# Hybrid conv/S5 block on one Trainium2 core: the u_s quarters are scaled, stored and reloaded one at a time, and the last g_s product moves ahead of two "so" products

## The chip, the cores and the metric

The kernel runs on one core of a Trainium2 chip. A core has four compute engines that run side by side, each with its own instruction stream in fixed order: TensorE (PE in the profile; its weight loads are shown as PEld), VectorE (DVE), ScalarE (ACT) and GpSimd (POOL). SyncE (SP) computes nothing here; it issues all DMA transfers of this kernel, also in fixed order, and a DMA whose data or buffer isn't ready holds what stands behind it in SP's stream. Engines wait for each other through semaphores.

The metric is device time in microseconds, lower is better. Three runs of the kernel before gave 844.75, 844.65 and 843.45 us, a median of 844.65 us.

## The reference

One decoder layer on x of shape 1024 x 1024, in float32. Cut to what matters:

```python
h = rms_norm(x, pre_g)
proj = h @ w_in
conv_in, z_c, u_s, z_s, g_c, g_s = split(proj)         # widths 2048, 1024, 512, 512, 1024, 1024
ca, cb = split(conv_in)
cu = causal_depthwise_conv(ca * sigmoid(cb), conv_w, conv_b)      # 31 taps
cu = silu(layer_norm(cu))
conv_out = (cu * silu(z_c)) @ w_conv_out
y = gelu(s5_mimo(u_s, ...))              # 32 groups of 16 channels, a 64-dim complex state each
y = y * sigmoid(y @ w_glu + b_glu)
ssm_out = (y * silu(z_s)) @ w_ssm_out
merged = sigmoid(g_c) * conv_out + sigmoid(g_s) * ssm_out
out = x + rms_norm(merged @ w_out, post_g)
```

The state recurrence of `s5_mimo` is linear: s_t = A s_(t-1) + B u_t, y_t = Re(C s_t) + D u_t.

## The kernel before, in words

**Tiling.** Activations lie as channel x time: a tile is 128 channels by 1024 time steps (4 KB in each partition, 512 KB in all). Every matrix product is done in three passes with operands split into a high and a low part (`h` and `l`, type fp32r): high times high, high times low, low times high. So a product with 8 blocks of 128 in its inner dimension ("a unit") is 48 matmuls of 128x128 by 128x512, and one with 4 blocks ("glu", "so") is 24. A weight comes in by DMA as a raw tile (`wload`, L687 to L694, two raw buffers), is copied to its high part by ScalarE (`wsplit_h`, L703), and the low part is the difference, taken by VectorE (`wsplit_l`, L711). When `wsplit_l` is done, the raw buffer is free, and the next `wload` is issued. The weights come in the order of the list `order`, two units ahead.

**Stages.** First come the normalisation and the products for u_s: three of its four 128-channel tiles together (L848), then the fourth (L867). A copy of each to SBUF is `usT[m]` (L185). Then the list `seq` (L757 to L761) gives the order of the products on TensorE: pairs `cb`, `ca` (convolution gate), `gc`, `zc`, `glu`, `zs`, pairs of `gs` and `so`, at last eight `co` products; after them comes the output product (L1017). What follows a product (sigmoid, multiplication, store) is put off by `post` and emitted by `flush` at step k = 1 of the next product (k = 0 with 4 blocks).

**u_s.** `us_out(m)` (L187 to L195) multiplies `usT[m]` by the norm factors on VectorE, stores it to the DRAM tensor `us_scratch` with one DMA of 512 KB, and reads it back in another layout with eight DMAs of 64 KB into `U[m]` (L195): 8 groups of 16 channels, 8 consecutive time steps folded into the partitions. The first of the eight reads must wait on SP until the store has landed. The function is called for m = 0 to 3 in a row, before the first product of `seq`.

**S5.** `s5_chain` first works out parameters (`s5_params`), then handles the four quarters (8 groups each) one after the other in `s5_quarter(c, P)`: it builds `RT` on VectorE (L392 to L396), transposes it on TensorE (`rp`, L399), multiplies it with `U[c]` (`ep`, L411), works out a small product `kp` (L432, L433), sines and cosines on ScalarE, a scan (L471), swaps halves of tiles through DMA (`E2`, `Zw`), and at the end has `yp` (L489, L490, which reads `U[c]` again), a GELU, a transpose `yq` (L497) and `y32[c]`.

**What sets the order.** All instructions are emitted by one Python program, and each engine runs its own in the order of emission. A planner, the object `clk` of class `Clock`, decides where side work goes: `clk.now` is the time planned for TensorE (1.296 us for each step k of a product), `clk.dve` the time up to which VectorE is planned to be busy. `clk.fg(cost)` adds cost to `clk.dve`. `clk.tick` moves `now` on and then runs one step of the first task in its list that is due (`max(t[1], self.dve) <= self.now`, L658), and starts over from the top of the list. A task is a generator that yields (cost, delay); with cost 0 the next due time is counted from its last due time. Tasks are `s5`, `conv` (the taps of the convolution, L537), `st` and `ln` (the layer norm), and `cu`.

**The "cu" entry.** The marker `("cu", 0)` in `seq` flushes what was put off, forces the convolution and the layer norm to be emitted, and adds a task with eight steps (L973, L974): each copies one tile to its high part (ScalarE) and takes the difference (VectorE). The first `co` product forces what is left of them (L981).

**Tiles.** Activation tiles come from one pool of 21 buffers (`NT = 21`, `T(name)`).

Of the kernel before, what the change touches and what calls it, by code (L numbers as in the profile page):

```python
# [35 lines left out]
def tile_hybrid_block(  # L36
# [40 lines left out]
    def T(name, dt=F32):  # L77
        return tp.tile([128, 1024], dt, tag="T", name=name)

    def PS(name, tag):  # L80
        return ps.tile([128, 1024], F32, tag=tag, name=name)

    def f32(t):
        return t.bitcast(F32)
# [76 lines left out]
    def x_spread(rb):  # L161
        for t in range(8):
            PE.matmul(rb[:, t * 128:(t + 1) * 128], lhsT=r8t[:, t:t + 1].to_broadcast([128, 128]), rhs=ident,
                      start=True, stop=True)
        rbc = T("rbc")
        A.activation(out=rbc, in_=rb, func=AF.Copy)
        return rbc
# [15 lines left out]
    def us_copy(m, p):  # L183
        usT[m] = T(f"usT{m}")
        A.activation(out=usT[m], in_=p, func=AF.Copy)  # L185

    def us_out(m, rbc):  # L187
        u = usT.pop(m)
        V.tensor_tensor(out=u, in0=u, in1=rbc, op=ALU.mult)
        clk.fg(1.2)  # L190
        nc.sync.dma_start(out=us_scr[m], in_=u)
        usU[m] = T(f"U{m}")
        src = us_scr[m].rearrange("(g h) (t n) -> t h g n", g=8, t=8)
        for t in range(8):
            nc.sync.dma_start(out=usU[m][16 * (7 - t):16 * (8 - t)].rearrange("p (g n) -> p g n", g=8), in_=src[t])  # L195
# [321 lines left out]
    def conv_taps(c, ext):  # L517
        acc[c] = T(f"acc{c}")
        av = acc[c].rearrange("p (i e n) -> p e i n", i=4, e=2)
        ye, yo = av[:, 0], av[:, 1]  # L520
        pp = T(f"pp{c}").rearrange("p (e i n) -> p e i n", e=2, i=4)
        p0, p1 = pp[:, 0], pp[:, 1]

        def src(e, r):
            a_, b_ = divmod(r, 4)
            return ext[:, e, 3 - b_:7 - b_, 4 - a_:132 - a_]

        A.activation(out=p0, in_=src(0, 0), func=AF.Copy, scale=cw[:, c, 0:1])  # L528
        A.activation(out=p1, in_=src(1, 0), func=AF.Identity, scale=cw[:, c, 1:2], bias=nb1[:, c:c + 1])
        A.activation(out=yo, in_=src(2, 0), func=AF.Copy, scale=hs[:, c, 0:1])  # L530
        yield 0.0, 2.2
        for r in range(1, 16):
            for e, o, w in ((0, p0, cw[:, c, 2 * r:2 * r + 1]), (1, p1, cw[:, c, 2 * r + 1:2 * r + 2]),
                            (2, yo, hs[:, c, r:r + 1])):
                if e == 1 and r == 15:
                    continue
                V.scalar_tensor_tensor(out=o, in0=src(e, r), scalar=w, in1=o, op0=ALU.mult, op1=ALU.add)  # L537
                yield 0.665, 0
        V.scalar_tensor_tensor(out=ye[:, 1:4, :], in0=p0[:, 1:4, :], scalar=b2[:, c:c + 1], in1=p1[:, 0:3, :],
                               op0=ALU.add, op1=ALU.add)  # L540
        V.scalar_tensor_tensor(out=yo, in0=p0, scalar=-1.0, in1=yo, op0=ALU.mult, op1=ALU.add)
        yield 1.2, 0
        V.scalar_tensor_tensor(out=ye[:, 0, 1:128], in0=p0[:, 0, 1:128], scalar=b2[:, c:c + 1],
                               in1=p1[:, 3, 0:127], op0=ALU.add, op1=ALU.add)
        V.tensor_scalar(out=ye[:, 0, 0:1], in0=p0[:, 0, 0:1], scalar1=chn[:, 0, c:c + 1], scalar2=None,
                        op0=ALU.add)
        V.tensor_tensor(out=yo, in0=yo, in1=p1, op=ALU.subtract)
        yield 1.1, 0
# [3 lines left out]
    def conv_chain():  # L552
        while conv_left[0]:
            if not conv_q:
                yield 0.0, 0.5
                continue
            c, e = conv_q[0]
            for v in conv_taps(c, e):
                yield v
            conv_q.pop(0)  # L560
            conv_left[0] -= 1
            clk.add(f"st{c}", ln_stat(c))
            yield 0.0, 0.0
# [8 lines left out]
    def ln_stat(c):  # L572
        yield 0.0, 3.5
        p = PS(f"lnp{c}", "aux")
        for t in range(8):
            PE.transpose(p[:, t * 128:(t + 1) * 128], acc[c][:, t * 128:(t + 1) * 128], ident)  # L576
        clk.now += 0.9
        yield 0.0, 2.0
        for t in range(8):
            V.bn_stats(out=st8[:, t, c, :], in_=p[:, t * 128:(t + 1) * 128])  # L580
            if t % 4 == 3:
                yield 0.9, 0.0
        stat_left[0] -= 1
        yield 0.0, 0.0
# [86 lines left out]
    clk = Clock()  # L671
# [80 lines left out]
    pairs = [[("cb", c), ("ca", c)] for c in range(8)]  # L752
    fill = [("gc", m) for m in range(8)] + [("zc", m) for m in range(8)]
    zs, glu = [("zs", m) for m in range(4)], [("glu", m) for m in range(4)]
    gso = [[("gs", m), ("so", m)] for m in range(8)]
    gc, zc = fill[0:8], fill[8:16]
    seq = pairs[0] + gc[0:1] + pairs[1] + gc[1:8] + pairs[2] + zc[0:2] + pairs[3] + zc[2:4]  # L757
    seq += [("yhl", 0)] + glu + zs[0:1] + pairs[4] + zs[1:4] + [("y2", 0)] + pairs[5] + gso[0] + gso[1] + pairs[6]
    seq += gso[2] + gso[3] + pairs[7] + zc[4:6] + gso[4] + zc[6:8] + gso[5] + gso[6] + gso[7][0:1] + [("cu", 0)]
    seq += gso[7][1:2]  # L760
    seq += [("co", m) for m in range(8)]  # L761
    NOW = ("yhl", "y2", "cu")
    order += [("us", 3)] + [u for u in seq if u[0] not in NOW] + [("wo", k) for k in range(WHL)]
# [17 lines left out]
    def s5_chain():  # L781
        yield from s5_params(P5)
        for c in range(4):
            while not P5_ready[0]:
                yield 0.0, 0.5
            yield from s5_quarter(c, P5)
        for c in range(4):
            yh[c], yl[c] = T(f"yh{c}", F32R), T(f"yl{c}", F32R)
            A.activation(out=yh[c], in_=y32[c], func=AF.Copy)
            V.tensor_tensor(out=yl[c], in0=y32[c], in1=f32(yh[c]), op=ALU.subtract)  # L790
            yield 1.15, 0
        s5_done[0] = True
        yield 0.0, 0.0
# [9 lines left out]
    rbc = None  # L803
    for k in range(8):
        if k == 0:
            us_weights(2)
            load_xt(6)
            load_xt(7)
            for t in range(3):
                load_x(t)  # L810
            clk.add('s5', s5_chain())
# [32 lines left out]
        for n_, (m, i) in enumerate([(m, i) for i in range(3) for m in range(3)]):  # L844
# [8 lines left out]
            if k == 6 and n_ == 5:  # L853
                rbc = x_spread(PS("rb", "aux"))
# [19 lines left out]
            wsplit_l()  # L874
        clk.tick(1.296)
    us_copy(3, usp[3])
    for m in range(4):
        us_out(m, rbc)
    P5_ready[0] = True
    clk.add('conv', conv_chain())  # L880

    mgh, mgl = {}, {}
# [15 lines left out]
    for u in seq:  # L898
        kind, m = u
# [244 lines left out]
```

## Time and profile before

| quantity | value |
|---|---|
| median of three runs | 844.65 us (843.45 to 844.75) |
| the profiled execution's own time | 844.35 us |
| span in the trace of that execution | 842.6 us |
| TensorE busy | 819.7 us, 97% of the span |
| weight loads busy | 681.1 us, 81% |
| VectorE busy | 622.1 us, 74% |
| ScalarE busy | 279.6 us, 33% |
| GpSimd busy | 25.8 us, 3% |
| DMA | 90.77 MB, 108 GB/s on average |
| mean granted TensorE clock | 0.994 |

Times in the trace count from the start of the span. An engine's row in a timeline has its start, its length, the source line, the operation with its output and inputs, how often it was repeated, and in brackets the idle time of the engine before it and what ended this. "SPq" is a DMA being issued by SP: its length is that of the issue, and the landing comes later. A list of waits sums idle time of an engine by the line that waited and the line that released it. The table of windows gives busy time of each engine in a stretch, and the clock that TensorE was granted as a share of full speed.

### The profile page before, as it was taken

Reading aid. Unit: us, or ns where it says so; the run is one execution under the profiler, and the core shown is the slowest. Engines: PE = TensorE matmul, PEld = TensorE weight load, DVE = VectorE, ACT = ScalarE, POOL = GpSimd, SP = SyncE. Lnnn points to the kernel's source line nnn. Section 1 sums busy time; section 2 is a strip of 40 time slices with the busy share of each in tenths; the row PEclk is TensorE's granted clock in tenths of the full one; section 3 lists DMA queues with packets and bytes.
Section 4 is the critical chain, followed back from the end, with each engine's and each line's share of the span. In section 5 each row is a group of like instructions: output and inputs, shape, how many; then the busy total and the mean of one; then the engine's idle time right before and its main releaser. Section 6 shows DMA issues by size and latency. Waiting matters only on the chain.

```text
span 842.6 us, 9753 instructions
## 1 busy us (share of the span) xinstructions
PE 819.7 (97%) x3856; PEld 681.1 (81%) x3856; DVE 622.1 (74%) x902; ACT 279.6 (33%) x301; POOL 25.8 (3%) x26
## 2 busy tenths in 40 slices
PE   6999799999999999999999999999999999999996
PEld 5887588888888888888888888888888788888885
DVE  4689499889799899988889869589593644452242
ACT  5762344354515453323231121033162411122121
POOL 3400000000000000000000000000000000000010
PEclk9999899999999999999999999999999999999999
DMA  9704432332323302210112202112343443325142
GB/s 343 273 26 147 153 90 75 103 111 101 87 77 100 90 26 99 76 51 26 51 38 87 78 24 100 75 64 101 137 171 129 153 172 145 140 76 189 51 175 100
DMA packets 35181, 90.77 MB, mean 108 GB/s; under 512 B 8305, under 2 KB 13041, under 8 KB 35137
## 3 DMA queue, kind: packets, MB, share of 16 engines
q1 hardware_dynamic: 35136, 90.17, 31.2%
q8 instruction: 30, 0.49, 0.2%
q14 instruction: 15, 0.11, 0.0%
HBM read 65.90 MB, written 18.87 MB: 101 GB/s over the span
## 4 chain that ended last, share of the span: by engine, by line
PE 81%; DVE 10%; ACT 3%; DMA 2%; issue 2%; SPq 1%; DVEq 0%; POOLq 0%; ACTq 0%
PE pgs L736 10%; PE pzc L736 10%; PE pco L736 10%; PE po L1017 10%; PE pcb L736 8%; PE pca L736 8%; PE pzs L736 5%; PE pso L736 5%; PE usp L848 4%; PE pgc L736 4%; PE pgl L736 3%; DVE pp L537 1%; DVE xl L176 1%; DMA Zw<-Zs 1%; PE lnp L576 1%
## 5 line engine op out<-in xcount | busy, mean ns | idle before, releaser
L537 DVE SCALAR_TENSOR_TENSOR pp<-ext,cw,pp 128x512 f32<-128x512 f32 x232 | 165.4, 745 | 10.5 <-ACT pp L528 10.5
L537 DVE SCALAR_TENSOR_TENSOR acc<-ext,hs,acc 128x512 f32<-128x512 f32 x120 | 89.3, 744 | 0.0
L1017 PE MATMUL po<-wox,mgh 128*128 128x512 f32 x192 | 52.3, 389 | 0.0
L736 PE MATMUL pcb<-xh,wh_cb 128*128 128x512 f32 x128 | 40.7, 399 | 5.6 <-ACT wh_cb L703 5.6
L513 ACT ACTIVATE ext<-ext 128x1179 f32<-128x1179 f32 x8 | 9.5, 1190 | 104.7 <-DVE ext L512 104.7
L1017 PEld LDWEIGHTS po<-wox,mgh 128*128 128x128 f32 x192 | 36.0, 188 | 7.5
L736 PE MATMUL pca<-xh,wl_ca 128*128 128x512 f32 x128 | 39.7, 391 | 1.2 <-DVE wl_ca L711 1.1
L736 PE MATMUL pco<-cuh,wl_co 128*128 128x512 f32 x128 | 39.5, 390 | 1.3 <-DVE wl_co L711 1.3
L736 PE MATMUL pgc<-xh,wh_gc 128*128 128x512 f32 x128 | 40.5, 397 | 0.0
L736 PE MATMUL pcb<-xh,wl_cb 128*128 128x512 f32 x128 | 40.3, 396 | 0.0
L736 PE MATMUL pcb<-xl,wh_cb 128*128 128x512 f32 x128 | 40.3, 397 | 0.0
L736 PE MATMUL pzc<-xh,wh_zc 128*128 128x512 f32 x128 | 40.3, 396 | 0.0
L736 PE MATMUL pzc<-xh,wl_zc 128*128 128x512 f32 x128 | 39.6, 390 | 0.5 <-DVE Sx L482 0.5
L736 PE MATMUL pca<-xh,wh_ca 128*128 128x512 f32 x128 | 39.8, 392 | 0.1
L1033 DVE TENSOR_TENSOR o<-po,postg 128x1024 f32<-128x1024 f32 (+1 forms) x9 | 10.0, 1106 | 40.3 <-ACT q L1032 40.3
L736 PE MATMUL pgc<-xl,wh_gc 128*128 128x512 f32 x128 | 39.5, 390 | 0.0
L736 PE MATMUL pgs<-xh,wh_gs 128*128 128x512 f32 x128 | 39.5, 390 | 0.0
L736 PE MATMUL pzc<-xl,wh_zc 128*128 128x512 f32 x128 | 39.5, 390 | 0.0
L736 PE MATMUL pgc<-xh,wl_gc 128*128 128x512 f32 x128 | 39.5, 389 | 0.0
L736 PE MATMUL pca<-xl,wh_ca 128*128 128x512 f32 x128 | 39.4, 389 | 0.0
L736 PE MATMUL pco<-cuh,wh_co 128*128 128x512 f32 x128 | 39.4, 389 | 0.0
L736 PE MATMUL pco<-cul,wh_co 128*128 128x512 f32 x128 | 39.4, 389 | 0.0
(267 smaller groups left out, 1773.2 us busy)
## 6 DMA issues: line engine op xcount, KB each, us to landing
xt<-in_xt_dram SPq DMA_DIRECT2D x8, 512.0 KB, 6.3
xin<-in_x_dram SPq DMA_DIRECT2D x8, 512.0 KB, 9.8
wr_cb<-in_w_in_dram SPq DMA_DIRECT2D x8, 512.0 KB, 3.3
wr_ca<-in_w_in_dram SPq DMA_DIRECT2D x8, 512.0 KB, 3.2
wr_gc<-in_w_in_dram SPq DMA_DIRECT2D x8, 512.0 KB, 3.3
gc_scratch<-gct SPq DMA_DIRECT2D x8, 512.0 KB, 2.6
wr_zc<-in_w_in_dram SPq DMA_DIRECT2D x8, 512.0 KB, 3.2
zc_scratch<-zct SPq DMA_DIRECT2D x8, 512.0 KB, 2.6
```

Source lines behind the costliest of these rows:

```text
L176: V.tensor_tensor(out=xl[:, k, :], in0=xn, in1=f32(xh[:, k, :]), op=ALU.subtract)
L513: A.activation(out=ext[:, :, 0:3, 1:132], in_=ext[:, :, 4:7, 0:131], func=AF.Copy)
L537: V.scalar_tensor_tensor(out=o, in0=src(e, r), scalar=w, in1=o, op0=ALU.mult, op1=ALU.add)
L576: PE.transpose(p[:, t * 128:(t + 1) * 128], acc[c][:, t * 128:(t + 1) * 128], ident)
L736: PE.matmul(p[:, js(j)], lhsT=lhs[:, ks], rhs=rhs(k, j), start=st, stop=sp_)
L848: PE.matmul(usp[m][:, js_], lhsT=lhs[:, kk[m]], rhs=rhs[:, k, js_], start=(k == 0 and i == 0), stop=(k == 7 and i == 2))
L1017: PE.matmul(p[:, js(j)], lhsT=lhs[k][:, s], rhs=rhs[k][:, js(j)], start=st, stop=sp_)
L1033: V.tensor_tensor(out=o[:, s], in0=p, in1=pog[:, s], op=ALU.mult)
```

## The change

The edit has two parts.

1. `us_out` keeps the multiplication and the store. The eight reads become a function of their own, `us_in(m)`. Quarter 0 is scaled, stored and read where it was before. Quarters 1 to 3 are scaled and stored by a new task `us`, one per step, with due times 8 us apart. It stands in the task list after `s5` and ahead of `conv`. The reads of quarter c (1 to 3) are emitted at the start of `s5_quarter(c)`.
2. In `seq`, the last `gs` product (`gs` 7) stands ahead of the `so` products 6 and 7; the marker `cu` follows it, so both of these `so` products come between the marker and the first `co` product, where one did before.

```diff
@@ us_out
         V.tensor_tensor(out=u, in0=u, in1=rbc, op=ALU.mult)
         clk.fg(1.2)
         nc.sync.dma_start(out=us_scr[m], in_=u)
+
+    def us_in(m):
         usU[m] = T(f"U{m}")
         src = us_scr[m].rearrange("(g h) (t n) -> t h g n", g=8, t=8)
         for t in range(8):
@@ seq
-    seq += gso[2] + gso[3] + pairs[7] + zc[4:6] + gso[4] + zc[6:8] + gso[5] + gso[6] + gso[7][0:1] + [("cu", 0)]
-    seq += gso[7][1:2]
+    seq += gso[2] + gso[3] + pairs[7] + zc[4:6] + gso[4] + zc[6:8] + gso[5] + gso[6][0:1] + gso[7][0:1] + [("cu", 0)]
+    seq += gso[6][1:2] + gso[7][1:2]
     seq += [("co", m) for m in range(8)]
@@ s5_chain
         for c in range(4):
             while not P5_ready[0]:
                 yield 0.0, 0.5
+            if c:
+                us_in(c)
             yield from s5_quarter(c, P5)
@@ after the fourth u_s product
     us_copy(3, usp[3])
-    for m in range(4):
-        us_out(m, rbc)
+    us_out(0, rbc)
+    us_in(0)
+
+    def us_rest():
+        for m in range(1, 4):
+            us_out(m, rbc)
+            yield 0.0, 8.0
+
     P5_ready[0] = True
+    clk.add('us', us_rest())
     clk.add('conv', conv_chain())
```

## Prediction, made before the changed kernel was run

> **What bounds the kernel now.** I read the page first. TensorE is busy for 819.7 of 842.6 us, so nearly all of what an edit of order can win lies in the 22.9 us in which it isn't, or in which its clock is down.
>
> ```profile
> PE 819.7 (97%) x3856; PEld 681.1 (81%) x3856; DVE 622.1 (74%) x902; ACT 279.6 (33%) x301; POOL 25.8 (3%) x26
> ```
>
> The list of waits of TensorE names those that another engine or a DMA ended (total, times, longest):
>
> ```profile
> PE usp L848 <- ACT wush L132: 7.2, 1, 7.2
> PE pcb L736 <- ACT wh_cb L703: 5.6, 1, 5.6
> PE pco L736 <- DVE wl_co L711: 1.3, 1, 1.3
> PE pca L736 <- DVE wl_ca L711: 1.1, 1, 1.1
> PE pzc L736 <- DVE Sx L482: 0.5, 1, 0.5
> ```
>
> The 7.2 us are the start, which the change doesn't touch. Three waits are within its reach: 5.6, 1.3 and 1.1 us. What is behind the first shows in the timelines of SP and of the engines around 91 us (start, length, line, instruction, in brackets the idle time before it):
>
> ```profile
> 63.79 0.33 SPq L191 DMA_DIRECT2D us_scratch<-usT  x1
> 66.45 3.65 SPq L195 DMA_DIRECT2D U<-us_scratch  x8
> 70.20 0.37 SPq L191 DMA_DIRECT2D us_scratch<-usT  x1
> ...
> 84.14 0.34 SPq L191 DMA_DIRECT2D us_scratch<-usT  x1
> 87.77 3.62 SPq L195 DMA_DIRECT2D U<-us_scratch  x8
> 91.48 0.37 SPq L693 DMA_DIRECT2D wr_cb<-in_w_in_dram  x1
> ```
>
> ```profile
> 94.91 1.06 ACT L703 ACTIVATE wh_cb<-wr_cb 128x1024 fp32r<-128x1024 f32 x1 [10.81 <-DMA wr_cb<-in_w_in_dram]
> 96.00 1.23 DVE L711 TENSOR_TENSOR wl_cb<-wr_cb,wh_cb 128x1024 fp32r<-128x1024 f32 x1 [10.73 <-ACT wh_cb L703]
> 96.02 1.22 PE L736 MATMUL pcb<-xh,wh_cb 128*128 128x512 f32 x2 [5.58 <-ACT wh_cb L703]
> ```
>
> The reader is to see one queue. Each quarter of u_s costs SP a store, the wait until it has landed, and eight issues: about 7 us, four times, from 63.79 to 91.4 us. The weight of the second `cb` stands behind all four. So ScalarE idles 10.81 us, VectorE 10.73 us and TensorE 5.58 us.
>
> The idle time has a second price. The table of windows (busy time of PE, PEld, DVE, ACT and POOL, then clock, DMA share, GB/s) shows the clock at half after the gap:
>
> ```profile
> 84.00:96.00 12.00, 6.43 (x33) 5.08 (x31) 1.24 (x3) 1.19 (x3) 0.95 (x1) 0.95 0.56 187
> 96.00:101.30 5.30, 5.28 (x12) 4.12 (x13) 5.30 (x6) 3.71 (x5) 0.00 (x0) 0.50 0.42 158
> 103.10:106.00 2.90, 2.90 (x15) 2.19 (x13) 2.90 (x6) 1.97 (x2) 0.00 (x0) 1.00 0.14 31
> ```
>
> Twelve matmuls took 5.3 us at clock 0.50; at full clock they take half, so 2.65 us were lost.
>
> The Trainium skill (TensorE: Matmul & The Clock Gate, Part 1) says that after an idle window of about 3.4 us the clock falls to half, and that about 3.4 us of work bring it back. The trace agrees on the half, not on the length: it was down for 5.3 us. By the rule's 3.4 us the loss would be 1.7 us, and the sum below would come out 0.95 us higher; I keep the row.
>
> **Part one: the quarters of u_s.** What goes from the front is three multiplications on VectorE, three stores and 24 reads on SP. Nothing is saved in all: the same instructions come later.
>
> ```profile
> 62.55 4.63 DVE L189 TENSOR_TENSOR usT<-usT,rbc 128x1024 f32<-128x1024 f32 x4
> 67.09 1.22 DVE L711 TENSOR_TENSOR wl_ca<-wr_ca,wh_ca 128x1024 fp32r<-128x1024 f32 x1
> 68.36 0.72 PE L736 MATMUL pca<-xh,wl_ca 128*128 128x512 f32 x2 [1.12 <-DVE wl_ca L711]
> ```
>
> *First term, -1.12 us.* The low part of `ca` follows the multiplications at once. With three of four (4.63 x 3/4 = 3.5 us) gone from before it, it is ready 3.5 us sooner, and the wait of 1.12 us goes with 2.4 us to spare.
>
> *Second term, -5.58 us.* SP is free after the reads of quarter 0, at 66.45 + 3.65 = 70.1 us. The raw buffer that `wr_cb` needs is free when `wl_ca` ends (68.3 before, some 65 now). So the load goes out at about 70.1 instead of 91.48 us and lands at about 73.5 (91.48 to 94.91 is 3.4 us). ScalarE then reaches `wh_cb` when what stands ahead of it is done; that is the copy of `ext`:
>
> ```profile
> 82.91 1.19 ACT L513 ACTIVATE ext<-ext 128x1179 f32<-128x1179 f32 x1 [13.23 <-DVE ext L512]
> ```
>
> So `wh_cb` ends by 84.10 + 1.06 = 85.2 us. TensorE wants it at 96.02 - 5.58 - 1.12 = 89.3 us. The wait is gone with 4 us of cover; were the cover gone too, `wl_cb` would be late next, which VectorE has done by about 86.4 us for a use at 90.2.
>
> *Third term, -2.65 us*, the half clock, which falls with the gap.
>
> *Where the work goes.* By the planner's rule `s5` comes first whenever it is due, and it is due as soon as VectorE is planned free, except in its own delays. Counting the planner's costs by hand, the delay after `RT` of quarter 0 takes the first multiplication, the delay after `otmp` the second, the delay after `ta` the third: with products `gc` 0 and the second `cb`, at roughly 79 to 93 us. VectorE has the room, since it idled 10.73 us right there and the three need 3.5 us. What is queued behind them on VectorE are S5 and conv steps; `wl_cb` keeps the 4 us above. Each store waits on SP for its multiplication, emitted in the same step; behind it stand weight loads that have most of a unit until use.
>
> The reads, eight issues of 3.65 us, now stand at the start of quarters 1 to 3, past the weight loads and the stores of `gc`, `E` and `Zw`. They can delay a load by 3.65 us; loads go out two units ahead, and a unit of 24 or 48 matmuls takes 5.44 us or twice that. `U` itself must be there for `ep`. Quarter 2 is the tightest:
>
> ```profile
> 637.81 5.44 PE pso L736 x24
> 265.75 1.78 PE ep L411 x16
> 202.03 1.22 DVE L382 TENSOR_TENSOR RT<-PR,bb 128x1024 f32<-128x1024 f32 x1
> 202.14 0.33 SPq L693 DMA_DIRECT2D wr_ca<-in_w_in_dram  x1
> 207.54 1.04 ACT L401 ACTIVATE R<-rp 128x1024 f32<-128x1024 f32 x1 [1.24 <-PE rp L399]
> 212.07 1.03 ACT L416 ACTIVATE Et<-ep 128x1024 f32<-128x1024 f32 x1 [2.56 <-PE ep L411]
> DMA to landing us min/median/max: 2.2/2.5/3.3
> ```
>
> The reads would go out right behind `wr_ca`, at 202.5 us, be issued by 206.2 and land 2.5 us later (last row, the landing times of `U`), at 208.7. The other input of `ep`, `R`, is ready at 208.6. `ep` ended near 212.0 and takes about 1.8 us, so it began at 210.2. That leaves 1.5 us: no cost, with a bound of +1 us for each of three quarters if the order shifts. POOL has nothing moved past it.
>
> *Does VectorE follow?* TensorE would be 9.35 us earlier from 103 us on (1.12 + 5.58 + 2.65). From 96 to 164 us VectorE is nearly full:
>
> ```profile
> 96.00:164.00 68.00, 67.98 (x373) 57.23 (x374) 64.03 (x82) 27.12 (x28) 0.95 (x1) 0.96 0.32 97
> 164.87 0.28 DVE L446 TENSOR_TENSOR kr<-kp,dmt 16x128 f32<-16x128 f32 x1 [2.71 <-ACT kr L445]
> 230.67 1.23 DVE L711 TENSOR_TENSOR wl_ca<-wr_ca,wh_ca 128x1024 fp32r<-128x1024 f32 x1 [4.34 <-ACT wh_ca L703]
> 243.69 0.73 PE L736 MATMUL pzc<-xh,wl_zc 128*128 128x512 f32 x2 [0.55 <-DVE Sx L482]
> ```
>
> At 164.87 us it waits for `kr`, that is for TensorE's `kp`. Up to there it had idled 10.73 us, 4.0 us in the window (68.00 - 64.03, the start of the 2.71 us included) and the rest of the 2.71, 0.9 us: 15.6 us. With `kp` 9.35 us earlier it can still afford 6.2 us, and it had 1.8 us of other idle time (4.0 + 0.9 - 2.71 = 2.2 at most). So it follows with about 4 us to spare. From there to the wait of 0.55 us at 243.69 the chain of waits runs through VectorE, ScalarE and DMA, starting from `kp`; it moves as a whole. Since S5 stands in other places against the products, I allow new small waits: +0.3 us, with bounds -0.55 (the present one goes) and +4.5 (the first rival).
>
> **Part two: gs 7 ahead of so 6 and so 7.** Nothing is added or removed.
>
> ```profile
> 654.17 1.03 ACT L951 ACTIVATE gst<-pgs 128x1024 f32<-128x1024 f32 x1 [10.70 <-PE pgs L736]
> 655.09 1.05 ACT L703 ACTIVATE wh_co<-wr_co 128x1024 fp32r<-128x1024 f32 x1
> 657.12 3.50 DVE L974 TENSOR_TENSOR cul<-acc,cuh 128x1024 fp32r<-128x1024 f32 x3 [11.94 <-ACT cuh L973]
> 660.54 1.22 DVE L711 TENSOR_TENSOR wl_co<-wr_co,wh_co 128x1024 fp32r<-128x1024 f32 x1
> 661.81 0.50 PE L736 MATMUL pco<-cuh,wl_co 128*128 128x512 f32 x1 [1.33 <-DVE wl_co L711]
> 634.09 0.68 DVE L711 TENSOR_TENSOR wl_so<-wr_so,wh_so 128x512 fp32r<-128x512 f32 x1
> ```
>
> Now the last `so` (5.44 us) covers the sigmoid, `wh_co`, the first `cuh`, three `cul` and `wl_co`, and TensorE still waits 1.33 us. In the changed order the same chain comes after `gs` 7, but the weight behind the three `cul` is that of `so` 7, half as large: VectorE needs 0.68 instead of 1.22 us, and ScalarE, in the same ratio, 0.46 us less than 1.05. So `wl_so` ends at 660.54 - 0.46 + 0.68 = 660.76 for a use at 661.81 - 1.33 = 660.48: a wait of 0.3 us. By the planner's count `wl_co` then stands behind two `cul`, the multiplication of `so` 6 and another `cul` (4.6 us), so it ends at 660.7 + 4.6 + 1.2 = 666.5, for a use 5.44 us after 660.76, at 666.2: another 0.3 us. So the term is -1.33 + 0.6 = -0.7 us, between -1.33 (no wait) and +0.5 (each wait twice what I count, and one more).
>
> **Sum.** The profiled execution took 844.35 us (0.3 below the median of the runs, inside their spread). 844.35 - 1.12 - 5.58 - 2.65 - 0.7 + 0.3 = 834.6 us; with half of the 0.3 for the median, 834.8 us.
>
> **Rivals.** *One: VectorE gives part of it back.* With TensorE earlier it must not idle more than 6.2 us up to `kp`; one more pair of waits as long as the 4.34 us at 230.67 (ScalarE held in its sine chain) makes 2.2 + 8.7 = 10.9, 4.7 too many. For it: VectorE is 94% busy there, and the interleaving is new. Against: since 106 us TensorE waited 0.55 us in all until 654. It gives 834.8 + 4.6 = 839.4 us. Chance 0.17.
>
> *Two: slower. The reads at a quarter's start come late.* SP takes its stream in order; if the buffer for `U` or a store ahead holds the reads for 5 us beyond what I found, `ep` waits, TensorE stands, and the loads behind are late too. The gap at 96 us shows the price of one such stop: 5.58 + 2.65 = 8.2 us. One stop gives 843.0, two of three quarters 851.2 us; it decides from about 10 us on. Against it: `R` takes as long as `U`, and the reads find their store landed for 40 us or more. Chance 0.05.
>
> The Trainium skill (DMA: Bandwidth & Descriptors, the section on the anatomy of one DMA) says that a wait for a semaphore takes place on the issuing sequencer before dispatch. The rows of SP above agree: the reads start at 66.45, 2.7 us after their store, and nothing else is issued in between.
>
> *Three: the change doesn't do what it says.* If a store of the new task comes to stand ahead of `wr_cb` on SP and its multiplication is late, the second and third terms stay: 844.35 - 1.12 - 0.7 = 842.5 us. Chance 0.04.
>
> **How the numbers follow.** Forecast 0.74 (in it, some 0.05 for a better result near 833), the rivals 0.17, 0.05, 0.04. The likeliest is 834.8 us. Low end: both unknowns at their good bound, 834.8 - 0.85 - 0.65, and 0.5 us of spread: 832.8. High end: the first rival and 1 us: 840.4. Beyond it lie two and three, and a larger give-back. A run tells no change from one of less than 0.2%, 1.7 us. Faster: 0.74 + 0.17 and most of three, 0.92. Same: 0.03. Slower: 0.05.
>
> **What would show it.** In the new trace: `wr_cb` issued near 70 us; no gap in TensorE near 90 us, and clock 1.00 from 84 to 106; `ep` of quarter 0 starting near 90 instead of 101.3; all three stores between 75 and 95 us; reads of `U` in four places; no wait of TensorE for `R` or `U`; two waits of some 0.3 us near 651 and 656 us. I'm wrong if TensorE shows a new wait of over 1 us between 95 and 330 us, above all at `ep` or `Sx`.

## The result, and the profile after

| quantity | before | after |
|---|---|---|
| median of the runs of one comparison | 844.7 us (4 runs, 843.45 to 845.08) | 835.01 us (4 runs, 834.77 to 835.94) |
| profiled execution's own time | 844.35 us | 834.89 us |
| span | 842.6 us | 833.1 us |
| mean granted clock | 0.994 | 0.998 |

The changed kernel is faster: ratio 0.989, interval 0.9873 to 0.9907. The median came out 0.2 us from the 834.8 us on record. How much of that is understanding and how much is errors that cancelled is the matter of the sections below.

The page of the changed kernel shows the same work in a shorter span (busy us, share, instructions):

```profile
PE 816.3 (98%) x3856; PEld 678.2 (81%) x3856; DVE 622.6 (75%) x902; ACT 279.4 (34%) x301; POOL 26.4 (3%) x26
```

The counts of TensorE, VectorE, ScalarE and GpSimd are those of before, so nothing was removed. TensorE's 3.4 us less of busy time are mostly matmuls that no longer run at half clock.

TensorE's waits on other engines in the changed kernel (total, times, longest):

```profile
PE usp L852 <- ACT wush L132: 7.2, 1, 7.2
PE pgs L738 <- ACT gst L962: 1.2, 1, 1.2
PE lnp L578 <- DVE st L582: 0.7, 2, 0.5
PE pso L738 <- DVE wl_so L713: 0.4, 1, 0.4
PE pgl L738 <- DVE wl_glu L713: 0.3, 1, 0.3
```

The start is untouched. The waits of 5.6, 1.3, 1.1 and 0.5 us of before (`wh_cb`, `wl_co`, `wl_ca`, `Sx`) are all gone. Behind the edit are four that were not there: 1.2 us at `gs` 6, 0.7 us in the layer norm, 0.4 us at an `so` and 0.3 us at the `glu` product.

SP's queue in the changed kernel, where the four blocks of store, wait and eight reads stood (start, length of the issue, line, transfer):

```profile
63.22 0.33 SPq L191 DMA_DIRECT2D us_scratch<-usT  x1
65.88 3.65 SPq L197 DMA_DIRECT2D U<-us_scratch  x8
69.62 0.38 SPq L695 DMA_DIRECT2D wr_cb<-in_w_in_dram  x1
...
80.45 0.33 SPq L191 DMA_DIRECT2D us_scratch<-usT  x1
86.91 0.33 SPq L191 DMA_DIRECT2D us_scratch<-usT  x1
91.19 0.56 SPq L191 DMA_DIRECT2D us_scratch<-usT  x1
121.95 3.79 SPq L197 DMA_DIRECT2D U<-us_scratch  x8
178.10 3.80 SPq L197 DMA_DIRECT2D U<-us_scratch  x8
234.20 4.00 SPq L197 DMA_DIRECT2D U<-us_scratch  x8
```

The load of `wr_cb` goes out at 69.62 instead of 91.48 us, right behind the reads of quarter 0. The other three stores follow their multiplications at 80 to 92 us, and the other reads stand about 56 us apart, one block for each quarter of S5. What this did on the engines, from the timelines of ScalarE and VectorE and the table of windows (busy time of PE, PEld, DVE, ACT, POOL, then clock, DMA share, GB/s):

```profile
83.44 1.04 ACT L705 ACTIVATE wh_cb<-wr_cb 128x1024 fp32r<-128x1024 f32 x1
...
187.56 1.03 ACT L403 ACTIVATE R<-rp 128x1024 f32<-128x1024 f32 x1 [2.02 <-PE rp L401]
```

```profile
63.11 1.22 DVE L713 TENSOR_TENSOR wl_ca<-wr_ca,wh_ca 128x1024 fp32r<-128x1024 f32 x1
79.21 1.22 DVE L189 TENSOR_TENSOR usT<-usT,rbc 128x1024 f32<-128x1024 f32 x1
85.66 1.22 DVE L189 TENSOR_TENSOR usT<-usT,rbc 128x1024 f32<-128x1024 f32 x1
89.27 1.22 DVE L189 TENSOR_TENSOR usT<-usT,rbc 128x1024 f32<-128x1024 f32 x1
```

```profile
84.00:96.00 12.00, 12.00 (x85) 10.12 (x84) 9.60 (x10) 6.18 (x9) 0.03 (x1) 1.00 0.65 214
96.00:101.30 5.30, 5.30 (x25) 4.40 (x24) 5.22 (x7) 4.03 (x4) 0.00 (x0) 1.00 0.20 36
```

The same two windows as before the change: TensorE is busy in all of 84 to 96 us, where it had 6.43 us, and the clock is 1.00 from 96 to 101.3, where it was 0.50. 25 matmul records instead of 12 fit into those 5.3 us.

The chain of waits of both kernels gives the gain up to that place. Before, then after (start, length, what, count):

```profile
37.31 1.78 PE rb L163 x16
101.50 1.88 PE ep L411 x16
```

```profile
36.47 2.05 PE rb L163 x16
87.06 1.78 PE ep L413 x16
90.22 2.72 PE pcb L738 x12
```

In the kernel before, `ep` of quarter 0 ended at 101.50 + 1.88 = 103.38 us, and TensorE had done two steps of the second `cb` by then. With the change it has done `ep` and these two steps at 90.22 + 2.72 = 92.94 us. That is 10.44 us earlier. Of these, 0.57 us were there from the start: `rb` ended at 38.52 instead of 39.09 us, ahead of anything that was edited. The front of part one is therefore worth 9.87 us.

### The profile page after: what moved, and what is told of

Its sections match the earlier page's. It is cut to its first block, busy times and chain, and to the rows that moved or that the text cites. A ratio compares the mean times of both kernels' runs of the same rounds, so it can differ in the third digit from the quotient of the medians.

```text
span 833.1 us, 9759 instructions
## 1 busy us (share of the span) xinstructions
PE 816.3 (98%) x3856; PEld 678.2 (81%) x3856; DVE 622.6 (75%) x902; ACT 279.4 (34%) x301; POOL 26.4 (3%) x26
## 4 chain that ended last, share of the span: by engine, by line
PE 76%; DVE 16%; issue 3%; ACT 2%; DMA 2%; POOL 1%; SPq 0%; DVEq 0%; POOLq 0%; ACTq 0%
PE pgc L738 11%; PE pco L738 10%; PE po L1028 10%; PE pgs L738 9%; PE pcb L738 8%; PE pzc L738 8%; PE pca L738 8%; DVE pp L539 6%; PE pso L738 4%; DVE acc L539 3%; PE usp L871 1%; PE pgl L738 1%; DMA xt<-in_xt_dram 1%; DMA xin<-in_x_dram 1%; POOL spt L227 1%
## 5 line engine op out<-in xcount | busy, mean ns | idle before, releaser
L1000 DVE TENSOR_TENSOR sgr<-pco,sgr 128x1024 f32<-128x1024 f32 x8 | 9.8, 1224 | 40.1 <-PE pco L738 40.1
L738 PE MATMUL pgs<-xl,wh_gs 128*128 128x512 f32 x128 | 39.4, 389 | 0.0
```

The source lines that it names most:

```text
L738: PE.matmul(p[:, js(j)], lhsT=lhs[:, ks], rhs=rhs(k, j), start=st, stop=sp_)
L1000: V.tensor_tensor(out=sgt, in0=p, in1=sgt, op=ALU.mult)
```

## Experiments

Ratios are to the kernel before, measured on the same chip in the same comparison.

### The two parts apart

The first run has part one alone: the changed kernel with the old line of `seq`.

```diff
-    seq += gso[2] + gso[3] + pairs[7] + zc[4:6] + gso[4] + zc[6:8] + gso[5] + gso[6][0:1] + gso[7][0:1] + [("cu", 0)]
-    seq += gso[6][1:2] + gso[7][1:2]
+    seq += gso[2] + gso[3] + pairs[7] + zc[4:6] + gso[4] + zc[6:8] + gso[5] + gso[6] + gso[7][0:1] + [("cu", 0)]
+    seq += gso[7][1:2]
```

> Only the quarters of u_s are changed; the list of products is that of before. Theory 'queue': the gain comes from the weight of the second cb, which no longer stands behind four quarters on SP. In the trace of the changed kernel the order of the last products took one wait of 1.33 us away and brought one of 0.37 us, so without it the time is 835.0 + 0.96 = 836.0 us, with a wait of TensorE of about 1.3 us for wl_co, and the wait of 1.16 us at gs 6 still there, since it stands ahead of the part that differs. Rival 'swap pays for itself': the wait at gs 6 comes from the new order of the products; then it is gone here and the time is 834.8 us.

It took 836.2 us (836.06 to 836.37), ratio 0.9908, interval 0.9894 to 0.9921. Two rows of TensorE's timeline matter:

```profile
618.16 0.73 PE L738 MATMUL pgs<-xh,wh_gs 128*128 128x512 f32 x2 [1.16 <-ACT gst L962]
...
653.33 0.72 PE L738 MATMUL pco<-cuh,wl_co 128*128 128x512 f32 x2 [1.33 <-DVE wl_co L713]
```

The old wait at `co` is back, as it should be. The new wait at `gs` 6 is here too, with its full 1.16 us, so it comes from part one and not from the order of the `so` products. It costs more than its length: the `so` product ahead of it begins 9.93 us earlier than in the kernel before (611.40 against 621.33 us), the one behind it only 8.48 us earlier (629.17 against 637.65), a loss of 1.45 us.

The second run has part two alone: the kernel before with the new lines of `seq`, the same diff the other way round.

> Only the order of the last gs and so products is changed. Theory: 844.7 - 0.96 = 843.7 us, wait for wl_so about 0.4 us, none for wl_co, and no wait at gs 6. Rival 'swap pays for itself': a wait of about 1.2 us at gs 6 appears here too, 844.9 us.

It took 842.91 us (842.22 to 844.65), ratio 0.9988, interval 0.9979 to 0.9998: 1.2 us less, with 0.2 to 1.8 inside the interval. In its trace the 1.33 us at `co` are gone and one wait has come:

```profile
PE pso L736 <- DVE wl_so L711: 0.4, 1, 0.4
```

There is no wait at `gs` 6 and none at `co`. By these two waits part two is worth 1.33 - 0.37 = 0.96 us; the execution that was profiled was the slowest of the eleven, with 6.37 us of wait at the second `cb`. Almost all of the gain is part one's.

### What in part one carries it

Part one does two things: it takes reads out of SP's queue ahead of a weight, and it makes three multiplications a task. First the task stays, and each quarter is read right behind its store (on top of part one alone):

```diff
@@ s5_chain
-            if c:
-                us_in(c)
@@ us_rest
             us_out(m, rbc)
+            us_in(m)
             yield 0.0, 8.0
```

> As part one alone, but the eight reads of each quarter follow its store at once, inside the new task, as before. Theory 'queue': what matters is only that the weight of the second cb goes out ahead of quarters 1 to 3; SP is held for some 7 us three times between 80 and 101 us, and the weights behind have cover: 836.0 us, within 0.7. Rival 'late reads': the reads behind their store push wr_gc and wr_ca by 7 to 14 us, TensorE waits 3 to 6 us and its clock falls: 839 to 844 us.

It took 839.71 us (838.58 to 841.06), ratio 0.9949, interval 0.9936 to 0.9962. That is inside the 839 to 844 us of the rival 'late reads', but not by its way: no wait for a weight is new and the clock did not fall. What came late was a transfer of S5 itself. SP's queue, then the instruction that it held on VectorE:

```profile
102.86 3.87 SPq L197 DMA_DIRECT2D U<-us_scratch  x8
107.32 5.30 SPq L455 DMA_DIRECT2D Mt<-kr  x8
113.34 0.51 SPq L476 DMA_DIRECT2D Zw<-Zs  x1
```

```profile
119.67 1.23 DVE L384 TENSOR_TENSOR Zw<-Zw,tk 128x1024 f32<-128x1024 f32 x1 [6.56 <-DMA Zw<-Zs]
```

The reads share the queue with the transfers `Mt` and `Zw` of quarter 0. The swap `Zw` goes out at 113.34 us, 4.3 us later than the 109.00 us of part one alone. VectorE stands for 6.56 us, and TensorE later for 1.9 us at `rp` and 0.6 us at `yq`, which part one alone does not show. So moving the reads to the quarters' starts is worth 839.71 - 836.2 = 3.5 us by the medians, though not by way of the weights, which the rival had. The trace is of the fastest of the five executions, 838.58 us; these two waits, 2.5 us, are nearly all of the 2.7 us by which its span exceeds that of part one alone.

Then the reverse: the reads at the quarters' starts, the multiplications and stores back at the front (again with the old `seq`):

```diff
     us_out(0, rbc)
     us_in(0)
-
-    def us_rest():
-        for m in range(1, 4):
-            us_out(m, rbc)
-            yield 0.0, 8.0
-
+    for m in range(1, 4):
+        us_out(m, rbc)
     P5_ready[0] = True
-    clk.add('us', us_rest())
```

> Part one without the task: all four multiplications and stores stand at the front as before, the reads of quarters 1 to 3 at the start of their quarter. Theory 'queue': SP is free from about 72 us, the weight of the second cb goes out then, and only the wait of 1.12 us for wl_ca stays: 836.0 + 1.1 = 837.1 us. Rival 'VectorE front': the 3.5 us of multiplications taken out of the front are what brings the gain; then 840 us or more here.

It took 834.53 us (834.07 to 835.07), ratio 0.9889, interval 0.9873 to 0.9904. I had expected 837.1, because the wait of 1.12 us at `wl_ca` comes back. It does come back, and still the run is 1.7 us below part one alone, with ranges that do not meet. TensorE's waits:

```profile
PE pco L738 <- DVE wl_co L713: 1.3, 1, 1.3
PE pca L738 <- DVE wl_ca L713: 1.1, 1, 1.1
```

The waits at `gs` 6, in the layer norm and at `glu` are not there. Up to 611 us the two kernels are level: the `so` product ahead of `gs` 6 begins at 611.47 us here and at 611.40 us in part one alone, so the 1.1 us at `wl_ca` cost about as much as the waits at `glu` and in the layer norm. The next `gs` begins at 633.23 us against 634.61: the difference of the spans, 1.4 us, arises at `gs` 6. So the late reads carry the gain, and the task gives some of it away.

How the task does it shows in TensorE's timeline, in the starts of `ep` of the four quarters and of the first five transposes of the layer norm `lnp` (us):

| kernel | `ep`, quarters 0 to 3 | `lnp`, first five |
|---|---|---|
| before | 101.30, 155.76, 210.09, 265.59 | 259.65, two at 377.52, 380.64, 434.61 |
| changed (with the task) | 86.89, 139.86, 191.47, 244.43 | 275.70, 325.19, 420.19, 422.78, 424.36 |
| this run (without it) | 92.85, 147.18, 201.50, 255.72 | 249.79, two at 367.65, 370.78, 424.74 |

Without the task S5 and the layer norm move forward with TensorE, by 8 to 10 us. With it S5 comes 14 to 21 us earlier and passes steps of the convolution: from 60 to 200 us VectorE runs 52 of these in the changed kernel and 65 in this run. The transposes then stand elsewhere, three of them within 5 us at 420 us, where the waits in the layer norm are. At `gs` 6 the wait can be followed on ScalarE, in the changed kernel (first two rows) and in this run:

```profile
613.35 1.25 ACT L624 ACTIVATE acc<-acc,chn 128x1024 f32<-128x1024 f32 x1 [2.28 <-DVE acc L623]
616.86 1.02 ACT L962 ACTIVATE gst<-pgs 128x1024 f32<-128x1024 f32 x1
611.50 1.25 ACT L624 ACTIVATE acc<-acc,chn 128x1024 f32<-128x1024 f32 x1 [2.89 <-DVE acc L623]
615.00 1.03 ACT L957 ACTIVATE gst<-pgs 128x1024 f32<-128x1024 f32 x1
```

The sigmoid `gst` that `gs` 6 waits for stands on ScalarE behind a step of the layer norm (`acc`), which waits for VectorE. With the task this step comes 1.85 us later. How the planner's choices lead from the early S5 to just these places I did not follow step by step.

### One load past the reads

If the queue is the cause, one instruction moved in the kernel before should bring most of the gain. In the next three runs the load of `wr_cb` goes out ahead of the last 8, 4 or 1 of the 32 reads; all else is as before.

```diff
@@ us_out
-        for t in range(8):
+        def read(t):
             nc.sync.dma_start(out=usU[m][16 * (7 - t):16 * (8 - t)].rearrange("p (g n) -> p g n", g=8), in_=src[t])
+        for t in range(8):
+            if m == 3 and t >= 0:    # 4 and 7 in the other two
+                late.append(lambda t=t: read(t))
+            else:
+                read(t)
@@ wload, behind the load
+            if u == ("cb", 1):
+                while late:
+                    late.pop(0)()
```

> The kernel before, with one thing moved: the load of the weight of the second cb is issued on SP after the store of quarter 3 and ahead of its eight reads. By the rows of before SP would issue it at 84.5 instead of 91.48 us, it lands at 87.9, wh_cb ends near 89.0, and TensorE wants it at 90.4. Theory 'queue and clock': the wait of 5.58 us goes, and with it the half clock (2.65 us): 844.7 - 8.2 = 836.5 us (up to 1 us more if small waits come). Rival 'only the idle time counts': the clock falls anyway: 839.1 us.

> As load_past_8_reads, but the load stands ahead of the last four reads only: issued 1.86 us earlier than before (89.6 us), wait of TensorE about 3.7 us. Theory 'the clock falls after any wait of this size': -1.86 us, half clock stays: 842.8 us. Rival 'threshold': a wait of 3.7 us no longer brings the half clock: 840.2 us, granted clock 1.00 after the gap.

> As load_past_8_reads, but ahead of the last read only: issued 0.47 us earlier than before, wait of TensorE about 5.1 us, half clock after it. Both theories: 844.7 - 0.5 = 844.2 us. It gives the first point of the row 1, 4, 8: with the clock proportional to the gap the time falls evenly, with a threshold it falls in one step of 2.65 us.

| run | median | ratio, interval | load issued | TensorE's wait |
|---|---|---|---|---|
| past 8 reads | 836.81 us (835.77 to 838.46) | 0.9907, 0.989 to 0.9924 | 84.29 us | 0.87 us |
| past 4 reads | 842.61 us (842.11 to 844.11) | 0.9983, 0.9973 to 0.9993 | 89.74 us | 6.26 us |
| past 1 read | 843.77 us (842.87 to 845.33) | 0.9993, 0.9984 to 1.0002 | 90.72 us | 6.63 us |

Past all eight, the row of the product reads:

```profile
91.15 0.73 PE L746 MATMUL pcb<-xh,wh_cb 128*128 128x512 f32 x2 [0.87 <-ACT wh_cb L713]
```

The wait falls from 5.58 to 0.87 us and the clock stays at 1.00 in the table of windows from 91.15 to 100 us. By the rows of before the gain is 5.58 + 2.74 - 0.87 = 7.45 us (2.74 is half of the 5.48 us at half clock, below); measured are 844.19 - 836.81 = 7.4 us (the interval of the ratio allows 6.4 to 9.3). One load moved past one wait and eight issues is worth about three quarters of the whole change.

Past four reads or one I expected the wait to shrink with each read. In the traces it did not. The load goes out earlier but takes longer while the reads move: from issue to the start of `wh_cb`, 5.35 us past four and 4.87 us past one, against 3.43 us in the kernel before and 3.74 us in part two alone, whose front is the same. The waits are even longer than before; less work falls into the spell at half clock (below), and the two balance. The run past four reads has a median 1.6 us lower all the same. Its trace cannot explain that: the profiled execution took 844.11 us, the slowest of its ten, and the waits of the others are not on record. Where the 1.6 us come from stays open.

### VectorE's room

The first rival of the prediction rested on VectorE having only some 4 us to spare. Two kernels add work there that leaves everything as it is: 3 or 8 extra VectorE operations behind the last multiplication, each the maximum of a tile and itself.

```diff
             us_out(m, rbc)
+            if m == 3:
+                for _ in range(3):    # 8 in the other
+                    V.tensor_tensor(out=rbc, in0=rbc, in1=rbc, op=ALU.max)
             yield 0.0, 8.0
```

> The changed kernel with three extra VectorE instructions of 1.14 us (3.4 us, results not used) right after the multiplication of quarter 3, unknown to the planner. The prediction found about 4 us to spare for VectorE up to kp of quarter 1. Theory 'spare': nothing or at most 0.5 us, 835.0 to 835.5. Rival 'VectorE is the bound already': the chain of waits of the changed kernel runs through VectorE from 287 us on, so nearly all comes out at the end: 838.0 us.

> As dve_plus_3 with eight instructions (9.1 us). Theory 'spare of about 4 us': some 5 us come out, 840 us. Rival 'bound already': 843.5 us, and more with the half clock. If VectorE had more room than thought: under 837 us.

With three (3.4 us more) the kernel took 835.38 us (835.0 to 835.7), ratio 0.9902, interval 0.9887 to 0.9917, with the same list of waits: nothing lost that can be measured. With eight it took 841.18 us (840.65 to 842.05), ratio 0.9969, interval 0.9958 to 0.9981. VectorE's timeline, the wait of TensorE and the windows behind it:

```profile
90.32 10.04 DVE L889 TENSOR_TENSOR rbc<-rbc 128x1024 f32<-128x1024 f32 x8
```

```profile
107.92 0.73 PE L738 MATMUL pca<-xh,wl_ca 128*128 128x512 f32 x2 [3.84 <-DVE wl_ca L713]
```

```profile
104.08:107.92 3.84, 0.00 (x1) 0.00 (x1) 3.77 (x5) 1.15 (x1) 0.00 (x0) 1.00 0.19 26
107.92:109.30 1.38, 1.38 (x6) 1.16 (x7) 1.38 (x3) 1.32 (x2) 0.00 (x0) 1.00 0.41 66
109.40:112.70 3.30, 3.30 (x9) 2.57 (x8) 3.27 (x4) 3.27 (x4) 0.00 (x0) 0.50 0.63 152
```

10.04 us more of work became 3.84 us of wait: 6.2 us were to spare up to this `wl_ca`. The 4 us that I had worked out were for another place, `kp` of quarter 1, and this run does not measure them: TensorE itself was late from here on. The wait and half of the 3.4 us at half clock make 5.5 us, of the 5.7 us by which the span grew. The waits at `gs` 6, in the layer norm and at `glu` are as long as without the extra work. A VectorE that is late near 95 us does not make them longer. That says nothing of its load near 318 us, since it had caught up long before: from 170 to 250 us it is busy for 72.19 us in the changed kernel and with three extra operations alike.

A third kernel takes the multiplications of quarters 1 to 3 off VectorE and gives them to GpSimd (their cost in the planner goes too):

```diff
-        V.tensor_tensor(out=u, in0=u, in1=rbc, op=ALU.mult)
-        clk.fg(1.2)
+        if m:
+            G.tensor_tensor(out=u, in0=u, in1=rbc, op=ALU.mult)
+        else:
+            V.tensor_tensor(out=u, in0=u, in1=rbc, op=ALU.mult)
+            clk.fg(1.2)
```

> The changed kernel, with the multiplications of quarters 1 to 3 on GpSimd, which idles there, instead of VectorE. Theory 'VectorE is the next bound': the small waits that are new in the changed kernel (1.16 us at gs 6, 0.66 at lnp, 0.29 at glu) come from VectorE being late, 3.5 us less work there takes most of them away: 833.2 us. Rival 'slack': VectorE has its room elsewhere and the waits come from the order: 835.0 us. A third way: GpSimd slows VectorE's instructions while it runs: 835 to 837 us, with longer VectorE rows between 80 and 95 us.

It took 841.37 us (840.91 to 841.65), ratio 0.9959, interval 0.9946 to 0.9971, some 6 us slower than the changed kernel. GpSimd's timeline and VectorE's beside it:

```profile
44.79 5.75 POOL L190 TENSOR_TENSOR usT<-usT,rbc 128x1024 f32<-128x1024 f32 x2 [8.93 <-ACT usT L185]
61.89 7.19 POOL L190 TENSOR_TENSOR usT<-usT,rbc 128x1024 f32<-128x1024 f32 x1 [11.35 <-ACT usT L185]
```

```profile
42.97 1.28 DVE L170 SCALAR_TENSOR_TENSOR xt<-xt,gcol,rbc 128x1024 f32<-128x1024 f32 x1
...
48.20 3.42 DVE L170 SCALAR_TENSOR_TENSOR xt<-xt,gcol,rbc 128x1024 f32<-128x1024 f32 x1
...
66.63 0.21 DVE L220 TENSOR_TENSOR ptb<-PI 128x64 f32<-128x64 f32 x1
66.87 2.30 DVE L220 TENSOR_TENSOR PR<-pta,ptb 128x64 f32<-128x64 f32 x1
```

VectorE's operations that run while GpSimd multiplies take 3.42 instead of 1.28 us and 2.30 instead of some 0.2 us. The first of them moves the low part of the first `cb` weight from 53.97 us in the changed kernel to 56.21, and TensorE waits 2.05 us for it, up to 57.48 us. Behind the wait TensorE ran at half clock from 58.6 to 61.9 us, and the product took 14.85 us instead of 10.88. Waits of 0.8 us at another `wl_cb`, 1.0 us each at `ep` and `yq` and 0.4 us at `rp` come on top, none of which the changed kernel has. So GpSimd does hold VectorE, as the third way had it, but earlier, at 48 and 67 us, and the time lies far above its 835 to 837 us. The waits at `gs` 6, in the layer norm and at `glu` are absent here, in a third interleaving; whether less work on VectorE or the other order removed them, this run does not tell.

### Putting together what paid

This kernel has the reads at the quarters' starts, the multiplications at the front, and the new `seq`: it is the changed kernel without its task.

> reads_late_only with the new order of the last gs and so products: the changed kernel without its task, all four multiplications at the front. Theory 'the two parts add, and the task costs': 834.5 - 0.96 = 833.6 us, 1.4 us faster than the changed kernel; waits of TensorE: 1.1 us for wl_ca, 0.4 for wl_so, none at gs 6, lnp, glu. Rival 'the task is free': the difference of reads_late_only to part one alone was chance; then 835.0 us.

It took 834.16 us (833.93 to 834.46), ratio 0.9883, interval 0.9867 to 0.99. Its waits beside the start are 1.1 us at `wl_ca` and 0.4 us at an `so`, as expected. The time is 0.6 us above the 833.6 us expected; in the profiled execution `rb` ended 0.5 us later than in the run with the old `seq`, which would answer for most of it. It is 0.85 us below the changed kernel, which was measured in another comparison; 1.4 us were expected.

The last kernel also removes the wait at `wl_ca` in the plain way, by order: the low part of `ca` and the load behind it come ahead of the multiplications of quarters 1 to 3. (`rest` is a list, empty at first; its definition is left out.)

```diff
@@ the step that makes the low part of a weight
             wload()
+            if u == ("ca", 0):
+                while rest:
+                    us_out(rest.pop(0), rbc)
@@ after the fourth u_s product
     us_in(0)
-    for m in range(1, 4):
-        us_out(m, rbc)
+    rest.extend((1, 2, 3))
     P5_ready[0] = True
```

> reads_late_swap with the low part of the ca weight, and the load behind it, ahead of the multiplications of quarters 1 to 3 on VectorE; the order is otherwise the same on every engine. Theory: the wait of 1.12 us for wl_ca goes and nothing takes its place: 833.6 - 1.1 = 832.5 us. Rival 'given back': TensorE meets VectorE's S5 chain 1.1 us earlier, and new waits at Sx or gs take it back: 833.6 us.

It took 832.5 us (831.89 to 833.01), ratio 0.9864, interval 0.9849 to 0.9878. That is the time expected, partly by luck: the kernel that it starts from was 0.6 us slower than expected, and the step gave 1.7 us instead of 1.1. Its list of waits:

```profile
PE pso L741 <- DVE wl_so L713: 0.4, 1, 0.4
PE po L1025 <- DVE wl_wo L713: 0.2, 1, 0.2
```

The start aside, 0.6 us of such waits are left. It beats the kernel before by 1.4%, and the kernel of the line above, on the same chip, by 1.7 us with ranges that do not meet. The changed kernel was measured in another comparison; its median is 2.5 us higher, and the intervals of the two ratios overlap between 0.9873 and 0.9878.

## Why the prediction was right, step by step

Each step against what the traces showed:

- **First term, -1.12 us at `wl_ca`.** Right in mechanism, 0.3 us too small. `wl_ca` starts at 63.11 instead of 67.09 us, and no wait for it is left. But from the first matmul of `ca` to the first of `gc` TensorE took 78.48 - 66.17 = 12.31 us before and 76.48 - 65.60 = 10.88 us after, 1.43 us less. In steady flow each pair of matmuls begins 0.45 us behind the last though it lasts 0.62 us, and idle time is counted from its end; the first pairs behind the wait then follow at 0.57 and 0.47 us.
- **Second term, -5.58 us at `wh_cb`.** Right, mechanism and place. The load goes out at 69.62 us (70.1 predicted) and `wh_cb` ends at 84.48 us (85.2 predicted). The run with one load past eight reads shows the cause alone.
- **Third term, -2.65 us of half clock.** Right in kind, a little small: 2.74 us, since the spell ended at 101.57 us and not at 101.3. Together the three make 9.44 us and the chain shows 9.87; 0.3 of the remaining 0.4 us are those of the first term.
- **Where the work goes.** The three multiplications came at 79.21, 85.66 and 89.27 us, in the stretch of 79 to 93 us that I had counted. The stores follow between 80 and 92 us. `ep` of quarter 0 started at 86.9 us, 3 us earlier than I said; it stands ahead of the second `cb` now.
- **The reads cost nothing.** Right: no wait for `U` anywhere. In quarter 2 the last read is issued by 181.9 us and, with the 2.5 us of landing in the rows of before, there by 184.4 us (an estimate); `R` is ready at 188.6 us. I had named it the tightest place, with 1.5 us to spare; it has some 4 us against `R`. The place itself was wrong: I had `ep` of quarter 2 move with TensorE, by 9.35 us, and it moved by 18.6.
- **VectorE follows.** Right in that TensorE did not wait for it up to `kp`, and 3.4 us more of work cost nothing. The 4 us to spare were not measured at their place; the run with eight extra operations shows 6.2 us at an earlier one. That the chain from `kp` moves as a whole with TensorE was wrong: S5 moved by 14 to 21 us.
- **New small waits, +0.3 us.** This is the term that was mis-sized. It came to -0.55 (`Sx`, gone) + 0.29 + 0.66 + 1.16 = +1.56 us, inside its bounds. The prediction allowed for S5 in other places against the products but not for the convolution falling behind it and the layer norm shifting, and two of these waits lie in the layer norm or behind a step of it. The rows that I looked at ended at 244 us; the three new waits lie at `glu` near 318 us, in the layer norm near 424 us and at `gs` 6 near 618 us, all far from the edit. The kernels with the multiplications at the front have none of them.
- **Part two, -0.7 us.** -0.96 us. The wait at `wl_so` came as 0.37 us for 0.3, at 646.70 us; the second one, 0.3 us at `wl_co`, did not.

The sum: -9.87 - 0.96 + 1.56 and the 0.57 us that the profiled run was ahead from the start make -9.84 us, for a measured difference of the spans of 9.5 us; the 0.3 us between them are about what `gs` 6 cost beyond its wait (1.45 against 1.16 us in part one alone). The prediction had -9.35 - 0.7 + 0.3 = -9.75. So that the median was met to 0.2 us is partly luck, errors that cancelled: 1.3 us too little for new waits against 0.8 us too little gained and 0.57 us from the start.

**The rivals.** That VectorE gives part back did not happen up to `kp`, the stretch that the rival named, nor in its size; some 2 us were given back later, at `glu`, in the layer norm and at `gs` 6, behind steps of VectorE. That late reads make it slower did not happen either. The run that kept reads behind the stores shows what a badly placed block of reads costs, 3.5 us, and that it strikes S5's own transfers first. That `wr_cb` would stand behind a store of the task did not happen, since it went out 11 us ahead of the first of them.

## What to carry to other kernels

On an in-order DMA queue, a store whose result is read back costs everything behind it the landing time as well as the issues; put the read where its consumer starts, and look first for the one load that stands behind such a wait, because moving that load alone may bring most of the gain. When work is handed to a planner rather than placed by hand, look at the waits of the whole kernel afterwards: here the new ones came some 230 to 530 us later, 2.1 us in all, and a kernel with an explicit order at the front, which has none of them, was 2.5 us faster (measured in another comparison). A wait in TensorE costs more than its length where the clock falls behind it, so price a gap by its length and half of the work in the spell that follows. In these traces the clock fell for waits of 2.05 us and more, the start aside, and not for those of 1.95 us and less; these are a handful of waits, not a threshold.

## What was not expected of the hardware

**The spell at half clock has two lengths, and it can start after the wait.** The windows of the kernel before, cut at the edges of the spell (clock third from the end):

```profile
94.80:96.02 1.22, 0.00 (x1) 0.01 (x1) 0.02 (x1) 1.11 (x2) 0.00 (x0) 0.50 0.57 228
96.02:101.50 5.48, 5.48 (x13) 4.32 (x14) 5.48 (x7) 3.69 (x5) 0.00 (x0) 0.50 0.44 167
101.50:101.60 0.10, 0.10 (x3) 0.10 (x2) 0.10 (x1) 0.00 (x0) 0.00 (x0) 0.70 1.10 451
```

And with the load past four reads:

```profile
93.60:100.40 6.80, 4.20 (x10) 3.33 (x11) 4.22 (x5) 4.80 (x6) 0.00 (x0) 0.50 0.55 161
```

Before, the clock fell about 94.75 us, 4.3 us into the wait, and was back at 101.57: 6.8 us. Past four reads it fell earlier in the wait and lasted as long, so only 4.2 us of work lay in it and a longer wait cost no more in all (6.26 + 2.1 against 5.58 + 2.74 us). With eight extra VectorE operations, above, TensorE waited 3.84 us at full clock, worked for 1.4 us at full clock, and then had it halved for 3.4 us: half as long. With the multiplications on GpSimd it did the same behind a wait of only 2.05 us: 1 us at full clock, then 3.4 us at half. After the wait of 1.95 us of the run that kept reads behind the stores, and after shorter ones, it did not fall. The length also differs between executions of one kernel: in the six with eight extra operations the mean clock of the whole execution was 0.997 in the profiled one, 0.996 in one and 0.994 in four. Against the 0.998 of the changed kernel, 0.994 means some 6.7 us at half clock in 839 us (an estimate from these means), so by this estimate most of them had a longer spell than the one in the trace.

The Trainium skill (TensorE: Matmul & The Clock Gate, Part 1) describes a free-running window of 4096 cycles, about 3.4 us, in which activity is watched. Spells of one and of two such windows fit it, if a window into which the idle time reaches does not count as busy; the loss of 1.7 us that the rule gives is right for the profiled run with eight extra operations and 1 us short for the kernel before. If windows of that length end where the clock falls (an estimate), the one ahead of the fall held 2.0 us of idle time with eight extra operations and 2.05 us with GpSimd's multiplications: it was not idle throughout.

**GpSimd's multiplications slow VectorE as well as themselves.** A 128x1024 multiplication took 2.9 us on average for the first two and 7.19 us for the third, where VectorE needs 1.22, and VectorE's own operations were held as shown. The second of them ended at 69.17 us, just behind GpSimd's third multiplication (69.08 us). The Trainium skill (GPSIMD Engine Reference, section 1, Specifications) says that the interfaces to SBUF are shared with VectorE, with contention where VectorE's instruction has two SBUF inputs. The operations that were held have two or more; by how much they are slowed only these rows tell.

**A load slows beside small strided reads.** The 512 KB load of `wr_cb` took 3.4 and 3.7 us to its use when it went out behind all the reads (before, and part two alone), and 4.9 and 5.4 us when one or four followed it. With all eight behind it it took 5.8 us, but it then also ran beside the store of quarter 3. These are single traces.
